# Feed-forward input of a two-layer model: tokens stationary, 512 weight columns moving, products in five units, values turned by VectorE and transfers

## The chip, the core and the metric

The kernel runs on one core of a Trainium2 chip. A core has TensorE (PE in the profile), VectorE (DVE), ScalarE (ACT), GpSimd (POOL) and SyncE (SP), which work beside one another, each through its own queue in order. The metric is the device time of one execution in microseconds. Before the change the median of three runs is 1403.25 us (1403.13 to 1403.97).

## The reference

512 tokens of width 1024 pass an attention layer, a feed-forward layer, an mLSTM layer, a second feed-forward layer and a last norm. All is float32. The change touches the first half of the feed-forward layers:

```
def rms_norm(x, g):
    y = xf * lax.rsqrt(jnp.mean(xf * xf, axis=-1, keepdims=True) + RMS_EPS)
    return y.astype(x.dtype) * g.astype(x.dtype)

def swiglu(xn, w_in, w_out):
    gu = xn @ w_in
    return (jax.nn.silu(gu[..., :D_FF]) * gu[..., D_FF:]) @ w_out

h = h + swiglu(rms_norm(h, ffn_norm[i]), ffn_w_in[i], ffn_w_out[i])
```

`w_in` has 1024 rows and 2 × 2816 columns (gates, then ups); `w_out` has 2816 rows and 1024 columns.

## The kernel before

Each float32 operand is split into a high part (written by ACT, `L207` for weights, `L225` for tokens) and a low part (DVE, `L208` and `L226`). A product is then three matmuls: high by high, high by low, low by high (`SPLITS`). A chunk of weights of 128x1024 numbers is loaded by SP, split, and held in one of three buffers for each of its raw, high and low forms (`W_BUFS`).

The residual `h` lies feature by feature: eight tiles `hx` (`hn` in layer 1) of 128 features by 512 tokens. `norm` (L1026) writes for each of the eight tiles the pair `n_h`, `n_l` (the tile times its gain, not yet divided by the root mean square) and its squares `n1sq`, which DVE adds into `n1ssum`. A step put off with `defer` multiplies `n1ssum` by ones on PE (`n1ss`, L1044), computes the inverse root, and a hook broadcasts it with two matmuls (`n1bc`, L328) into `rbc`, by which DVE later multiplies results.

`ffn_in` (L1057) computes gates and ups and their product `hid`, eleven tiles of two times 128 hidden values by 512 tokens. Weights are stationary and tokens move, so results stand hidden value by hidden value, as `ffn_out` wants them. Three column pairs (`PLAIN`) are plain products with 512 moving columns. The other eight column pairs are two-by-two blocks (gates and ups, upper and lower half of the features, two halves of the tokens), made with the seven products of Strassen's scheme in Winograd's form instead of eight (`PRODUCTS`): `A..` and `S..` are weight blocks and their sums (made by DVE, L1186), `B..` and `T..` token blocks and their sums, with 256 moving columns each.

`Halves` (L1297) does `ffn_out` in the same scheme, with three of the eleven tiles in plain products (`p0`, `p1`). Its weights are prepared two chunks ahead: `ffn_in` prepares with `AHEAD = 2`, and its last chunks already prepare the first of `ffn_out` (`unit.prepare`). `load` (L1311) brings a chunk with SP, or adds it to a buffer with an accumulating load of POOL (L1313).

A scheduler orders the instructions of each engine when the program is built, from the order of the code and its own estimate of times; the names of engines' rows below are as it left them. The following lines set the order of the chunks in `ffn_in`:

```
for n, (j, i) in enumerate(todo):
    prepare(n + AHEAD)
    if i == 0:
        steps_of = products(j, prepared[j][1])
    steps_of[i]()
```

The functions as they were:

Of the kernel before, what the change touches and what calls it, by code (L numbers as in the profile page):

```python
# [17 lines left out]
P = 128  # L18
# [52 lines left out]
def tile_hybrid_dilated_attn_mlstm(  # L71
# [954 lines left out]
    def norm(key, k0, name, gate=None):  # L1026
        pair = x_tiles(name)
        ssum = npl.tile([P, SEQ], F32, tag="ssum", name=name + "ssum")
        for k in range(KC):
            with tc.issue_after(gate) if gate is not None else nullcontext():  # L1030
                split_act(pair[0][k], pair[1][k], h[k], col(key, k0 + k))
                if k == 0:
                    nc.scalar.activation(ssum, h[k], AF.Square)
                else:
                    sq = npl.tile([P, SEQ], F32, tag="sq", name=name + "sq", bufs=2)
                    nc.scalar.activation(sq, h[k], AF.Square)
                    nc.vector.tensor_tensor(ssum, ssum, sq, op=ALU.add)
# [3 lines left out]
        def sums():  # L1041
# [5 lines left out]
            box["finish"]()  # L1047
        rbc, r, hook = inverse_rms(v, name, box)
        defer(1, sums)
# [3 lines left out]
    PRODUCTS = (("A11", "B11"), ("S1", "T1"), ("S2", "T2"), ("A12", "B21"), ("S3", "T3"), ("S4", "B22"), ("A22", "T4"))  # L1053
    PLAIN = 6
    AHEAD = 2

    def ffn_in(layer, fp, pair, rbc, hook, unit):  # L1057

# [4 lines left out]
        banks = itertools.cycle(("acc", "acc", "acc", "s", "s", "o", "o"))  # L1063

        def bank(name):
            tag = next(banks)
            return ps.tile([P, 512], F32, tag=tag, name=name, bufs=3 if tag == "acc" else 2)

        def place(i, name, dtype):
            p, tag = (xp, "x%d" % (i - 3)) if 3 <= i < 11 else (fp, "hid%d" % i)  # L1070
            return p.tile([P, 2, SEQ], dtype, tag=tag, name="f%d%s%d" % (layer, name, i))

        def hidden(i):
            return place(i, "hid", F32)

        def temp(tag, name, bufs=1):
            return fp.tile([P, SEQ], F32, tag=tag, name=name, bufs=bufs)

        def op_tile(i, name):
            return fp.tile([P, 4, HALF], F32R, tag="op%d" % i, name="f%d%s" % (layer, name))  # L1080


        ops, raw = {}, {}

        def split_tokens(key):
            i = [b for _, b in PRODUCTS].index(key)
            hi, lo = ops[key] = [op_tile(2 * i + part, key + "hl"[part]) for part in range(2)]
            nc.scalar.activation(hi, raw[key], AF.Copy)
            nc.vector.tensor_tensor(lo, raw[key], hi.bitcast(F32), op=ALU.subtract)

        def normalized():
            xs = [fp.tile([P, 4, SEQ], F32, tag="w8", name="f%dx%d" % (layer, i), bufs=2) for i in range(2)]
            for i in range(2):
                for t in range(2):
                    raw["B%d%d" % (i + 1, t + 1)] = xs[i][:, :, t * HALF:(t + 1) * HALF]
            for k in range(KC):
                nc.vector.scalar_tensor_tensor(xs[k // 4][:, k % 4], h[k], col("ffn", layer * KC + k), rbc,
                                               op0=ALU.mult, op1=ALU.mult)
                yield
            split_tokens("B11")  # L1100
            raw["T1"] = fp.tile([P, 4, HALF], F32, tag="t1", name="f%dt1" % layer)
            nc.vector.tensor_tensor(raw["T1"], raw["B12"], raw["B11"], op=ALU.subtract)
            yield

            raw["T3"] = raw["B12"]
            nc.vector.tensor_tensor(raw["T3"], raw["B22"], raw["B12"], op=ALU.subtract)
            split_tokens("T1")
            yield
            split_tokens("T3")
            yield  # L1110
            split_tokens("B22")
            yield
            raw["T2"] = raw["B22"]
            nc.vector.tensor_tensor(raw["T2"], raw["B22"], raw["T1"], op=ALU.subtract)
# [12 lines left out]

        def some(n):
            for _ in itertools.islice(steps, n):
                pass  # L1130


        chunks = [(j, ch, half) for j in range(0, PLAIN, 2) for ch in range(KC // 4) for half in range(2)]
        ready = []

        def split_next():
            if chunks:
                j, ch, half = chunks.pop(0)
                ready.append(split_chunk(weight_chunk(wi, ch, half * D_FF + j * P, 4, "f%dj%d_%d%d" % (layer, j, half, ch))))

        def plain(j):
# [4 lines left out]
            for ch in range(KC // 4):  # L1146
                for half in range(2):
# [804 lines left out]
```

## Time and profile before

| what | us |
|---|---|
| median of the runs | 1403.25 |
| profiled execution, its own time | 1403.12 |
| its span | 1401.3 |
| `ffn_in` of layer 0 on PE | from 489.10 to 717.09 |
| `ffn_in` of layer 1 on PE | from 1052.20 to 1280.63 |

The profile is one execution. A row of groups names line, engine, operation, `out<-in`, partitions by elements and the count, then busy time in us, mean of one in ns, and the idle time ahead of it with what ended it. A row of the chain has start, length and what. A row of the timeline has start, length, engine, line, and in brackets the idle time before it with its releaser. The span is the time from the first to the last instruction; the execution's own time has 1.8 us more around it. The granted clock of TensorE was 0.999.

### The profile page before, as it was taken

Reading aid. Unit: us, or ns where it says so; the run is one execution under the profiler, and the core shown is the slowest. Engines: PE = TensorE matmul, PEld = TensorE weight load, DVE = VectorE, ACT = ScalarE, POOL = GpSimd, SP = SyncE. Lnnn points to the kernel's source line nnn. Section 1 sums busy time; section 2 is a strip of 40 time slices with the busy share of each in tenths; the row PEclk is TensorE's granted clock in tenths of the full one; section 3 lists DMA queues with packets and bytes.
Section 4 is the critical chain, followed back from the end, with each engine's and each line's share of the span. In section 5 each row is a group of like instructions: output and inputs, shape, how many; then the busy total and the mean of one; then the engine's idle time right before and its main releaser. Section 6 shows DMA issues by size and latency. Waiting matters only on the chain.

```text
span 1401.3 us, 20914 instructions
## 1 busy us (share of the span) xinstructions
PE 1387.5 (99%) x8118; PEld 1226.5 (88%) x8118; DVE 1085.5 (77%) x1834; ACT 681.9 (49%) x1127; POOL 114.6 (8%) x161
## 2 busy tenths in 40 slices
PE   9999999999999999999999999999999999999997
PEld 7788888888888888999999988798888899999886
DVE  7976659687797687778798688987758778789865
ACT  7245553232325443444574554985534344457534
POOL 1014101000010100000012010100000000001322
PEclk9999999999999999999999999999999999999999
DMA  9538734427262423323586433221232432337762
GB/s 300 150 75 197 197 110 112 153 82 249 75 203 76 118 91 121 121 82 101 151 238 136 92 108 93 88 61 61 75 97 90 130 119 63 121 121 202 190 135 75
DMA packets 134379, 177.21 MB, mean 126 GB/s; under 512 B 7748, under 2 KB 98948, under 8 KB 134280
## 3 DMA queue, kind: packets, MB, share of 16 engines
q1 hardware_dynamic: 118320, 140.15, 32.0%
q0 software_dynamic: 13728, 33.86, 11.5%
q10 hardware_dynamic: 2232, 1.86, 0.5%
q8 instruction: 64, 1.05, 0.3%
q14 instruction: 35, 0.29, 0.1%
HBM read 162.19 MB, written 10.09 MB: 123 GB/s over the span
## 4 chain that ended last, share of the span: by engine, by line
PE 91%; DVE 6%; ACT 1%; issue 1%; DMA 0%; ACTq 0%; DVEq 0%
PE f1j_u L1215 5%; PE f0j_u L1215 5%; PE f1j L238 5%; PE f0j L238 5%; PE f0j_p L1215 3%; PE f1j_p L1215 3%; PE f0j_c L1215 3%; PE f1j_c L1215 3%; PE awo L238 3%; PE mwo L238 3%; PE mqk L238 3%; PE o_o L1476 2%; PE mo L238 2%; PE o_o L1880 2%; PE o_acc L1894 2%; PE o_s L1476 2%
## 5 line engine op out<-in xcount | busy, mean ns | idle before, releaser
L238 PE MATMUL f1j<-n_h,f1j_h 128*128 128x512 f32 x96 | 37.5, 390 | 0.0
L238 PE MATMUL f0j<-n_h,f0j_h 128*128 128x512 f32 x96 | 37.5, 390 | 0.0
L238 PE MATMUL f1j<-n_h,f1j_l 128*128 128x512 f32 x96 | 37.4, 389 | 0.0
L238 PE MATMUL f0j<-n_h,f0j_l 128*128 128x512 f32 x96 | 37.4, 389 | 0.0
L238 PE MATMUL f0j<-n_l,f0j_h 128*128 128x512 f32 x96 | 37.4, 389 | 0.0
L238 PE MATMUL f1j<-n_l,f1j_h 128*128 128x512 f32 x96 | 37.4, 389 | 0.0
L1313 POOL DMA_DIRECT2D o1own<-in_ffn_w_out_dram x8 | 9.8, 1238 | 286.9 <-DVE o1B L1360 258.5
L1313 POOL DMA_DIRECT2D o0own<-in_ffn_w_out_dram x8 | 10.2, 1309 | 265.7 <-PE f0j_u L1215 226.7
L523 DVE TENSOR_TENSOR rot<-rot,sinr 32x1024 f32<-32x1024 f32 x24 | 28.9, 1205 | 0.0
L238 PE MATMUL mo<-n_h,mo_k_h 128*128 128x512 f32 x64 | 25.4, 397 | 0.0
L238 PE MATMUL mo<-n_h,mo_k_l 128*128 128x512 f32 x64 | 25.2, 394 | 0.0
L238 PE MATMUL mo<-n_l,mo_k_h 128*128 128x512 f32 x64 | 25.2, 394 | 0.0
L238 PE MATMUL awo<-ao_h,awo_k_h 128*128 128x512 f32 x64 | 25.2, 396 | 0.0
L238 PE MATMUL mqk<-n_h,mqk_k_h 128*128 128x512 f32 x64 | 25.1, 392 | 0.0
L238 PE MATMUL mqk<-n_l,mqk_k_h 128*128 128x512 f32 x64 | 25.1, 392 | 0.0
L238 PE MATMUL awo<-ao_l,awo_k_h 128*128 128x512 f32 x64 | 25.0, 390 | 0.0
L238 PE MATMUL mqk<-n_h,mqk_k_l 128*128 128x512 f32 x64 | 25.0, 390 | 0.0
L238 PE MATMUL awo<-ao_h,awo_k_l 128*128 128x512 f32 x64 | 24.9, 392 | 0.0
L238 PE MATMUL mwo<-yo_h,mwo_k_h 128*128 128x512 f32 x64 | 24.9, 389 | 0.0
L238 PE MATMUL mwo<-yo_l,mwo_k_h 128*128 128x512 f32 x64 | 24.9, 389 | 0.0
L238 PE MATMUL mwo<-yo_h,mwo_k_l 128*128 128x512 f32 x64 | 24.9, 389 | 0.0
L1476 PE MATMUL o_o<-o0T,o0s_h 128*128 128x256 f32 x128 | 23.4, 285 | 0.0
(2319 smaller groups left out, 5413.8 us busy)
## 6 DMA issues: line engine op xcount, KB each, us to landing
f0j_w<-in_ffn_w_in_dram SPq DMA_DIRECT2D x28, 512.0 KB, 4.3
f1j_w<-in_ffn_w_in_dram SPq DMA_DIRECT2D x28, 512.0 KB, 4.0
o0a_w<-in_ffn_w_out_dram SPq DMA_DIRECT2D x12, 512.0 KB, 4.0
o1a_w<-in_ffn_w_out_dram SPq DMA_DIRECT2D x12, 512.0 KB, 8.6
awo_k_w<-in_attn_w_out_dram SPq DMA_DIRECT2D x8, 512.0 KB, 4.0
o0own<-in_ffn_w_out_dram POOLq DMA_DIRECT2D x8, 512.0 KB, 9.1
mv_k_w<-in_mlstm_w_in_dram SPq DMA_DIRECT2D x8, 512.0 KB, 4.2
mqk_k_w<-in_mlstm_w_in_dram SPq DMA_DIRECT2D x8, 512.0 KB, 3.6
```

Of the source, the lines that this page charges most:

```text
L238: nc.tensor.matmul(acc, whl[a][:, k, m * P:(m + 1) * P], pairs[b][kk], start=(kk == 0 and (a, b) == SPLITS[0]), stop=(kk == nk - 1 and (a, ...
L523: nc.vector.tensor_tensor(sh, sh, sinr.unsqueeze(1).to_broadcast([R, 2, SEQ]), op=ALU.mult)
L1215: nc.tensor.matmul(acc[name][:, m * HALF:(m + 1) * HALF], whl[a][:, k, m * P:(m + 1) * P], ops[okey][b][:, k], start=(fresh and m == 0 and ...
L1313: nc.gpsimd.dma_start(view, self.source(col, ch), accum_op=ALU.add)
L1476: nc.tensor.matmul(dst[m // 2][:, (m % 2) * HALF:(m % 2 + 1) * HALF], whl[a][:, k, m * P:(m + 1) * P], unit.form(okey, b, 2 * c + k), star ...
L1880: nc.tensor.matmul(dst[t], unit.form(okey, a, 2 * c + k)[:, t * P:(t + 1) * P], whl[b][:, k], start=(first and k == 0 and (a, b) == SPLITS ...
L1894: nc.tensor.matmul(rest[n][tb], unit.plain[c][a][k][:, tb * P:(tb + 1) * P], whl[b][:, k], start=(c == 0 and (n == 1 or tb >= 2) and k == ...
```

## The change

`norm` gets `rows=True` for the feed-forward layers. The tokens of a tile are then reordered as they are written: token 4x + o goes to column 128 o + x, so that each of four blocks of 128 columns holds every fourth token. The step between neighbouring numbers on one side of these instructions is 16 bytes. The inverse root stays a value per token (`r`, and `nr` with a minus), and `hook` and `rbc` are gone.

In `ffn_in` tokens are now stationary and weights move with 512 columns. First come four chunks `rest` for the last 256 gate and 256 up columns, in plain products over four token blocks. Then come five units of 512 gate and 512 up columns, each with seven products in two chunks of twelve matmuls. `a..` and `s..` are the weight blocks and sums: `begin` loads a11 and a21 and adds a22 to the latter with POOL's accumulating load; the others are made by DVE (L1120, L1123) and a further accumulating load (L1121). `token_forms` makes the token sums from scaled copies of `h`, `f0x` (L1144).

Results stand token by token. They are multiplied by `r` or `nr`, a value for each partition, and the product of gate and up must be turned for `ffn_out`: `turn` has DVE transpose blocks of 32x32 (L1181), written with a step of 16 bytes, and `spread` brings the blocks to their partitions, four by copies of POOL (L1188) and twelve by transfers of SP (L1190). The last unit is spread in two halves, 24 transfers. In `Halves`, tile 10 becomes the first plain one (`PLAIN_AT`), and some buffers move.

The diff, cut:

```diff
-    def norm(key, k0, name, gate=None):
+    by_rows = lambda t: t.rearrange("p (o x) -> p x o", o=TB)
+    by_time = lambda t: t.rearrange("p (x o) -> p x o", o=TB)
+    def norm(key, k0, name, gate=None, rows=False):
...
-                split_act(pair[0][k], pair[1][k], h[k], col(key, k0 + k))
+                split_act(to(pair[0][k]), to(pair[1][k]), of(h[k]), col(key, k0 + k))
...
-                    nc.scalar.activation(sq, h[k], AF.Square)
+                    nc.scalar.activation(to(sq), of(h[k]), AF.Square)
...
+        todo = [("rest", None, c) for c in range(KC // 2)] + [
+            (u, key, c) for u in range(UNITS) for key, _ in PRODUCTS for c in range(2)]
...
+            for c in range(2):
+                nc.sync.dma_start(quarter(raw["first", c]), weights(u, "a11", c))
+            for c in range(2):
+                nc.sync.dma_start(quarter(raw["own", c]), weights(u, "a21", c))
+                nc.gpsimd.dma_start(quarter(raw["own", c]), weights(u, "a22", c), accum_op=ALU.add)
...
+            if key == "s1":
+                nc.vector.tensor_tensor(own, own, first, op=ALU.add)
+                nc.gpsimd.dma_start(quarter(first), weights(u, "a21", c), accum_op=ALU.add)
+            elif key == "s2":
+                nc.vector.tensor_tensor(own, own, raw["a12", c], op=ALU.add)
...
+        def turn(to, o, src, n):
+            nc.vector.transpose(to.rearrange("p g n j o -> p o n g j")[:, o], src.rearrange("p (n x) -> p n x", n=n))
+        def spread(dest, src, first=0):
+            for a, g in itertools.product(range(TB), repeat=2):
...
+                if a == g:
+                    nc.gpsimd.tensor_copy(to, of)
+                else:
+                    nc.sync.dma_start(to, of)
...
+            else:
+                g = kept["g", t]
+                nc.vector.scalar_tensor_tensor(g, banks["u"][t], nr[:, t:t + 1], g, op0=ALU.mult, op1=ALU.mult)
+                turn(kept["to"], t, g, 4)
...
+                for t in range(2):
+                    for k in range(2):
+                        for a, b in SPLITS:
+                            nc.tensor.matmul(banks[name][t], tokens(dict(PRODUCTS)[key], a, 2 * c + k, t), whl[b][:, k],
...
-            if i % 2:
-                advance()
...
+            advance()
+            if n > 0:
+                next(forms, None)
...
+    PLAIN_AT = (10, 8, 9)
...
-                self.load(raw, place[0], place[1] + c)
+                self.load(raw, place[0], PLAIN_AT[c] if key[0] == "p" else place[1] + c)
```

Three places where the order of instructions moves. The first is ACT at the start of layer 0's feed-forward, from the first square on (`awo` are weights of the projection before, `hx` the residual's tiles). Before:

```order
L1033 ACTIVATE n1ssum<-hx_2836 128x512
L1036 ACTIVATE n1sq<-hx_2837 128x512
L207 ACTIVATE awo_k_h<-awo_k_w 128x1024
L1036 ACTIVATE n1sq<-hx_2838 128x512
L1036 ACTIVATE n1sq<-hx_2839 128x512
L207 ACTIVATE f0j_00_h<-f0j_00_w 128x1024
L1036 ACTIVATE n1sq<-hx_2840 128x512
L1036 ACTIVATE n1sq<-hx_2841 128x512
L225 ACTIVATE n_h_3903<-hx_2836,cols 128x512
L225 ACTIVATE n_h_3903<-hx_2837,cols 128x512
```

The same place after the change:

```order
L1037 ACTIVATE n1ssum<-hx_2836 128x128x4
L1040 ACTIVATE n1sq<-hx_2837 128x128x4
L1144 ACTIVATE f0x_4056<-hx_2836,cols 128x128x4
L1144 ACTIVATE f0x_4056<-hx_2837,cols 128x128x4
L207 ACTIVATE awo_k_h<-awo_k_w 128x1024
L1040 ACTIVATE n1sq<-hx_2838 128x128x4
L1040 ACTIVATE n1sq<-hx_2839 128x128x4
L1144 ACTIVATE f0x_4056<-hx_2838,cols 128x128x4
L207 ACTIVATE f0restNone_h<-f0restNone_w 128x1024
L1144 ACTIVATE f0x_4056<-hx_2839,cols 128x128x4
L1144 ACTIVATE f0x_4057<-hx_2840,cols 128x128x4
L1040 ACTIVATE n1sq<-hx_2840 128x128x4
```

Six scaled copies now stand among the squares. To the last square, from the `awo_k_h` just ahead of these rows on, the queue has 28 instructions: eight squares, six copies, eight `n_h` and six splits of 128x1024; before it had 21. On PE the matmuls of `n1ss` stand after 24 matmuls of the feed-forward layer in both programs.

The second is DVE where unit 1 of layer 0 ends and unit 2 begins (`f0u1` is unit 1, `f02a` are a11 and a12 of unit 2). Before, at the end of a column pair:

```order
L208 TENSOR_TENSOR f0j10A_l<-f0j_w_4842,f0j10A_h 128x1024
L1221 TENSOR_TENSOR f0j8g_4880<-f0j_p_4726,f0j8u_4781 128x512
L208 TENSOR_TENSOR f0j10S_l<-f0j10S,f0j10S_h 128x1024
L1254 TENSOR_TENSOR f0hid_4879<-f0j8v_4751,f0j8g_4880 128x2x256
L1186 TENSOR_TENSOR f0j10S<-f0j10S,f0j_w_4842 128x1024
L1258 TENSOR_TENSOR f0hid_4879<-f0j_u,f0j8g_4811 128x2x256
L208 TENSOR_TENSOR f0j10S_l<-f0j10S,f0j10S_h 128x1024
```

After:

```order
L1181 STREAM_TRANSPOSE f0u1turn<-f0u1up_4601 128x4x4x32
L1181 STREAM_TRANSPOSE f0u1turn<-f0u1up_4603 128x4x4x32
L208 TENSOR_TENSOR f02a_l<-f0u2w_4721,f02a_h 128x1024
L1235 SCALAR_TENSOR_TENSOR f0u1g_4561<-f0u_u,n1nr,f0u1g_4561 128x512
L1235 SCALAR_TENSOR_TENSOR f0u1g_4563<-f0u_u,n1nr,f0u1g_4563 128x512
L1181 STREAM_TRANSPOSE f0u1turn<-f0u1g_4561 128x4x4x32
L1181 STREAM_TRANSPOSE f0u1turn<-f0u1g_4563 128x4x4x32
L208 TENSOR_TENSOR f02a_l<-f02a_w,f02a_h 128x1024 x2
```

The two products (L1235) and two turns that end a unit now stand ahead of the low parts of the next unit's a12 (last row). POOL's four copies L1188 and SP's twelve transfers L1190 wait for the last of these turns.

The third is SP where `ffn_in` of layer 0 ends and `ffn_out` begins (`o0p_w` are the weight chunks of the first plain product p0, `o0own` and `o0first` other weights of `ffn_out`). Before:

```order
L1315 DMA o0first_6569<-in_ffn_w_out_dram 128x2x512 x2
L1315 DMA o0a_w<-in_ffn_w_out_dram 128x2x512 x3
L1315 DMA o0p_w<-in_ffn_w_out_dram 128x2x512
L1315 DMA o0own_6282<-in_ffn_w_out_dram 128x2x512
L1315 DMA o0own_6323<-in_ffn_w_out_dram 128x2x512
L1315 DMA o0p_w<-in_ffn_w_out_dram 128x2x512 x2
```

After:

```order
L1312 DMA o0first_5997<-in_ffn_w_out_dram 128x2x512
L1312 DMA o0p_w<-in_ffn_w_out_dram 128x2x512
L1190 DMA f0hid_5666<-f0u4turn 32x2x128 x12
L1190 DMA f0hid_5683<-f0u4turn 32x2x128 x12
L1312 DMA o0p_w<-in_ffn_w_out_dram 128x2x512 x2
L1312 DMA o0own_5786<-in_ffn_w_out_dram 128x2x512 x2
```

The 24 transfers of the last unit stand between the first and the second chunk of p0. In layer 1 the rows are the same (`o1p_w`, `f1u4turn`).

More of the change, by code (lines that the diff above doesn't have):

```diff
@@ L1047, in sums, with finish @@
             box["finish"]()
+        defer(1, sums)
+        if rows:
+            r, nr = (npl.tile([P, TB], F32, tag="rtok", name=name + n, bufs=2) for n in ("r", "nr"))
+            def finish():
+                nc.vector.tensor_scalar(v, v, 1.0 / D, EPS, op0=ALU.mult, op1=ALU.add)
+                rsqrt_newton(npl, v, TB, name + "r", r)
+                nc.vector.tensor_scalar(nr, r, -1.0, None, op0=ALU.mult)
+            box["finish"] = finish
+            return pair, r, nr
         rbc, r, hook = inverse_rms(v, name, box)
-        defer(1, sums)
@@ L1050, in norm, with ffn_in @@
         return pair, rbc, r, hook
-    PRODUCTS = (("A11", "B11"), ("S1", "T1"), ("S2", "T2"), ("A12", "B21"), ("S3", "T3"), ("S4", "B22"), ("A22", "T4"))
-    PLAIN = 6
+    PRODUCTS = (("a11", "B11"), ("a12", "B21"), ("s1", "T1"), ("s2", "T2"), ("s3", "T3"), ("s4", "B22"), ("a22", "T4"))
+    UNITS = D_FF // 512
     AHEAD = 2
-    def ffn_in(layer, fp, pair, rbc, hook, unit):
+    def ffn_in(layer, fp, pair, r, nr, unit):
         wi = ffn_w_in[layer]
[L1063 to L1102, printed above, removed]
@@ new lines, in prepare @@
+        def prepare(n):
+            if n >= len(todo):
+                unit.prepare(n - len(todo))
+                return
+            u, key, c = todo[n]
+            name = "%s%s%s%d" % (nm, u, key, c)
+            if u == "rest":
+                src = wp.tile([P, 1024], F32, tag="wraw", name=name + "_w", bufs=W_BUFS)
+                for half in range(2):
+                    c0 = half * D_FF + UNITS * 512
+                    nc.sync.dma_start(src.rearrange("p (k g n) -> p k g n", k=2, g=2)[:, :, half],
+                                      wi[2 * c * P:2 * (c + 1) * P, c0:c0 + 256].rearrange("(k p) n -> p k n", p=P))
+                made[n] = split_chunk((src, 1024, quarter, name))
+                return
+            if (key, c) == ("a11", 0):
+                begin(u)
+            first, own = raw["first", c], raw["own", c]
+            if key in ("a12", "a22"):
+                src = raw[key, c] = wp.tile([P, 1024], F32, tag="wraw", name=name + "_w", bufs=W_BUFS)
+                nc.sync.dma_start(quarter(src), weights(u, key, c))
+            else:
+                src = first if key in ("a11", "s3") else own
+            made[n] = split_chunk((src, 1024, quarter, name))
+            if key == "s1":
[3 more added lines that the diff above has]
+                nc.vector.tensor_tensor(own, own, raw["a12", c], op=ALU.add)
@@ L1261, in ffn_in @@
[L1261 to L1275 removed]
+            nc.vector.tensor_tensor(half1(x2), half2(x2), half1(x2), op=ALU.subtract)
@@ new lines, in ffn_in, with rest_out @@
+        hid = unit.hid = [None] * (FC // 2)
+        def rest_out(accs):
+            hid[-1] = fp.tile([P, 2, SEQ], F32, tag="hid10", name=nm + "hid10")
+            to = turned(2, "rest")
+            for o in range(TB):
+                g = wide(("g2", "up")[o // 2], "gr%d" % o, 256)
+                nc.scalar.activation(g, accs[o][:, :256], AF.Silu, scale=r[:, o:o + 1])
+                nc.vector.scalar_tensor_tensor(g, accs[o][:, 256:], r[:, o:o + 1], g, op0=ALU.mult, op1=ALU.mult)
+                turn(to, o, g, 2)
+            spread(hid[-1], to)
@@ L1469, in tile_hybrid_dilated_attn_mlstm @@
                        25: (("T4", 3),)}, {"p1": 3}, ("a22",), ("s2",))
-        ffn_in(0, fp, pair, rbc, hook, unit)
+        ffn_in(0, fp, pair, r, nr, unit)
         whole = {}
```

306 lines of the change are left out of this document (139 added, 167 removed).

## The prediction

> **What bounds the kernel now.** I read the page first, then the chain that ended last, then the two feed-forward inputs by windows. The page says that TensorE never rests and that its clock is whole:
>
> ```profile
> span 1401.3 us, 20914 instructions
> PE 1387.5 (99%) x8118; PEld 1226.5 (88%) x8118; DVE 1085.5 (77%) x1834; ACT 681.9 (49%) x1127; POOL 114.6 (8%) x161
> PEclk9999999999999999999999999999999999999999
> ```
>
> The windows below cut each layer's `ffn_in` into its plain pairs and its seven-product pairs, layer 0 and then layer 1. The columns are length, busy time of PE, weight load, DVE, ACT and POOL, clock, DMA share, GB/s:
>
> ```profile
> 489.10:555.82 66.72, 66.72 (x300) 55.33 (x300) 53.56 (x80) 26.36 (x31) 0.00 (x0) 1.00 0.36 111
> 555.82:717.09 161.27, 161.27 (x1347) 161.27 (x1346) 129.83 (x131) 85.23 (x109) 2.44 (x2) 1.00 0.40 116
> 1052.20:1118.92 66.72, 66.72 (x301) 55.33 (x300) 53.55 (x80) 26.35 (x31) 0.00 (x0) 1.00 0.36 111
> 1118.92:1280.63 161.71, 161.71 (x1350) 161.71 (x1349) 130.49 (x131) 85.51 (x110) 1.20 (x1) 1.00 0.36 110
> ```
>
> PE is busy in every microsecond of all four. So the stage costs what its matmuls cost, 227.99 us in layer 0 and 228.43 in layer 1, and anything that makes PE wait there is added in full. The chain gives the pace of each kind (start, length, what):
>
> ```profile
> 489.10 5.44 PE f0j L238 x24
> 494.54 0.79 PE n1ss L1044 x8
> 495.32 8.34 PE f0j L238 x36
> 503.66 0.47 PE n1bc L328 x2
> 558.70 2.88 PE f0j_p L1215 x24
> 847.17 10.90 PE mv L296 x48
> ```
>
> A matmul of 512 columns takes 5.44/24 = 226.7 ns and one of 256 columns 2.88/24 = 120 ns. The mv row has tokens stationary and weights moving, as the change has, and 512 columns: 10.90/48 = 227.1 ns. Turning the operands round is therefore free.
>
> **The matmuls.** Before, a layer has 288 of 512 columns and 1344 of 256: 65.3 + 161.3 us, and with the two small rows (0.79 and 0.47) that is the two windows. After, it has 96 for the rest and 5 × 7 × 24 = 840 for the units, all of 512 columns: 936 × 226.7 = 212.2 us. The four sums of n1ss stay (0.79), the broadcast n1bc goes. So 213.0 instead of 227.99 and 228.43: **−15.0 and −15.4, together −30.4 us**. What is late next is everything that feeds PE, at three places.
>
> **The head: squares behind more and slower work.** PE's order has n1ss after 24 matmuls, before and after, so PE waits there until the eighth square is summed. ACT's queue in layer 0, and what its instructions cost:
>
> ```profile
> 472.55 1.06 ACT L207 ACTIVATE awo_k_h<-awo_k_w 128x1024 fp32r<-128x1024 f32 x1 [2.04 <-PE awo L238]
> 491.19 0.62 ACT L1036 ACTIVATE n1sq<-hx 128x512 f32<-128x512 f32 x1
> L225 ACT ACTIVATE n_h<-hx,cols 128x512 fp32r<-128x512 f32 x8 | 5.3, 712 | 0.3 <-PE awo L238 0.3
> L1510 ACT ACTIVATE hn<-hx x4: 1129/1142/1147, 801.4 to 807.2; 128x512 f32<-128x512 f32 x4
> L1500 DVE TENSOR_TENSOR hn<-o_acc,hx x3: 1060/1064/1066, 819.6 to 827.0; 128x512 f32<-128x512 f32 x3
> L1037 DVE TENSOR_TENSOR n1ssum<-n1ssum,n1sq 128x512 f32<-128x512 f32 x7 | 4.8, 687 | 0.3
> ```
>
> Today the last square ends at 491.81, long before PE asks at 494.54. The change rewrites every square and every n_h with a step of 16 bytes, and puts six scaled copies f0x and a split of T1 ahead of the last square. L1510 and L1500 write with that step too: 1142 ns against the 620 of n1sq, and 1064 against the 687 of L1037. From 472.55 to the last square stand 22 stepped instructions and six splits of 128x1024. Eight n_h are busy for 5.3 us and not for 8 × 0.712, so instructions of a row overlap by some 0.08; at 1.06 and 0.97 us each the queue is 23.3 + 5.8 = 29.1 us and ends at 501.7 without a single wait; with waits on PE and DVE as in the timeline I take 503. The last sum (0.69) and n1ss (0.79) follow: PE goes on at about 504.5 instead of 495.32. **+9 us**, bounds 0 (stepped writes cost nothing extra) and 12 (with a wait of 2.04, as that of the first row, more).
>
> Layer 1 has its residual spread over 43 us, so most squares are early. From the first n_h:
>
> ```profile
> 1045.44 1.34 ACT L225 ACTIVATE n_h<-hn,cols 128x512 fp32r<-128x512 f32 x2 [2.66 <-PE mwo L238]
> 1056.03 0.69 DVE L1037 TENSOR_TENSOR n3ssum<-n3ssum,n3sq 128x512 f32<-128x512 f32 x1
> 1058.43 8.34 PE f1j L238 x36
> ```
>
> Behind 1045.44 stand eight n_h, two squares, one f1x and two splits: 11 × 1.06 + 1.9 = 13.6, so 1059.0; the sum and n3ss bring PE to 1060.6 if ACT is alone, and some 1.5 later with DVE's eight n_l at 1.06 between them. Against 1058.43: **+3 us**, bounds 0 and 6.
>
> **Inside the units.** A unit takes PE 168 × 0.2267 = 38.1 us. Its feeding, by these rows:
>
> ```profile
> L208 DVE TENSOR_TENSOR f0j_l<-f0j_w,f0j_h 128x1024 fp32r<-128x1024 f32 x5 | 6.1, 1222 | 1.1 <-ACT f0j_h L207 1.0
> L226 DVE SCALAR_TENSOR_TENSOR n_l<-hx,cols,n_h 128x512 fp32r<-128x512 f32 x8 | 5.8, 747 | 0.2 <-ACT n_h L225 0.2
> L870 DVE STREAM_TRANSPOSE a0pB<-a0p x2: 2162/2168/2173, 231.4 to 235.9; 128x1920 f32<-128x1920 f32 x2
> L876 POOL COPY a3pT<-a3pB x8: 575/580/588, 454.3 to 458.7; 32x480 f32<-32x480 f32 x8
> 1280.63:1311.10 30.47, 30.47 (x150) 25.40 (x149) 25.08 (x36) 16.92 (x26) 4.82 (x6) 1.00 0.96 273
> ```
>
> DVE: 14 splits and 4 sums at 1.22, 8 products at 0.75, 4 turns. L870 gives 1.13 ns an element, 0.58 us for 512, when it writes in one run; the new turns write with a step of 16 bytes, which no transpose of the trace does. Bounds 0.58 and, with L1510's 522 ns on top, 1.10; I take 1.0, since L1510 and L1500 have the step and L870 has not. Sum 22.0 + 6.0 + 4.0 = 32 of 38.1 us, so DVE keeps pace. DMA: 12 loads of 512 KB and 0.8 MB of turned values a unit, 7.1 MB in 38.1 us, 186 GB/s, below the 273 that the last row shows. The sums of weights that accumulating loads now make have these rows:
>
> ```profile
> L1313 POOL DMA_DIRECT2D o0own<-in_ffn_w_out_dram x8 | 10.2, 1309 | 265.7 <-PE f0j_u L1215 226.7
> o0own<-in_ffn_w_out_dram POOLq DMA_DIRECT2D x8, 512.0 KB, 9.1
> ```
>
> The tightest is that for s3: s1's split comes two chunks ahead of its matmuls, some 6 us after the unit's start, DVE's sum 1.2 later, 1.31 to issue, 9.1 to land: 17.6, and s3's split is due at 8 chunks of 2.72 less 2.3, at 19.5. All of these loads lie beside PE's work with some 2 us in hand and are charged nothing; where that is gone, each of ten units pays the lateness whole.
>
> The tight point is the **join of two units**. At a unit's end E, DVE does two products and two turns, then the low part of the next a12's first chunk; PE wants it after a11, 24 × 0.2267 = 5.44 us later. The first product can start before E, so: E + 0.2 + 0.75 + 2.0 + 1.22 = E + 4.2, with semaphores up to 5.5. **+1 us** for all eight joins, bounds 0 and 20 (below).
>
> **The tail: loads behind the turned values.** After the last unit SP issues 24 transfers that wait for the last turn (E + 0.2 + 0.75 + 2.0 = E + 2.95), and only then the second and third weight chunks of p0. Rows:
>
> ```profile
> L878 SPq DMA_DIRECT2D a3pT<-a3pB x12: 507/592/824, 454.2 to 461.7; - x12
> o0p_w<-in_ffn_w_out_dram SPq DMA_DIRECT2D x6, 512.0 KB, 4.5
> 717.09 11.52 PE o_acc L1476 x96
> 734.08 1.36 PE o_acc L1490 x6
> 1280.63 2.75 PE o_acc L1880 x12
> 1294.70 1.39 PE o_acc L1894 x6
> ```
>
> E is 717.09 today, and the second chunk of p0 begins at 734.08, E + 17.0. 24 × 0.592 = 14.2 puts the load at E + 17.2, its landing (4.5) at 21.7, and a split of high (1.06) and low (1.22) part at E + 24.0: **+7 us**. Bounds: 0.507 each and a turn of 0.58 give 3.6; at the 0.66 that 8.01 us for twelve would make, 8.7. In layer 1 PE has the transposed residual in between: E is 1280.63, p0 begins at 1294.70 and its second chunk 5.44 later, E + 19.5, so 2.5 less: **+4.5**, bounds 1 and 6.5.
>
> **Sum**, against the profiled execution's own 1403.12 us (its span 1401.3; the median of the runs shown is 1403.25, nothing between them): −30.4 + 9 + 3 + 1 + 7 + 4.5 = −5.9, so **1397 us**. With head and tail 8 us better or worse together it is 1389 to 1405; 0.2%, 2.8 us, is what a measurement here can tell from no change.
>
> **Rivals.**
>
> (a) *The fillers cost little.* Stepped writes cost ACT and DVE nothing, the last square is as early as now, SP issues at 507 ns. For: ACT is idle 51% of the span. Against: L1510 and L1500 both show the step's price. Head 1, joins 0, tail 3.6 + 1: −24.8, **1378**.
>
> (b) *Slower: the joins are late.* Place: eight joins, where four POOL copies of 32 x 512 (0.58 each by L876, whose rows have 480) become due in the moment in which DVE must make the low part of a12. The trace has one such meeting:
>
> ```profile
> 1324.39 2.26 DVE L208 TENSOR_TENSOR o1s_l<-o1own,o1s_h 128x1024 fp32r<-128x1024 f32 x1
> 1324.15 1.42 POOL L1853 TENSOR_TENSOR ht<-ht,gbc 128x512 f32<-128x512 f32 x1 [1.62 <-ACT fsq L1852]
> ```
>
> A split that otherwise takes 1.22 us took 2.26 beside a POOL instruction. If all four copies go first, the low part comes at E + 4.2 + 2.3 = 6.5, with one more microsecond of its own 7.5: 1.1 to 2.1 beyond the 5.44; with the later semaphores of the term above 1.4 to 2.5. It decides from 5.44 on; eight times that is 11 to 20 us, so 1407 to 1416, **1411**. Against: a copy starts from a semaphore, the split stands on the same engine as the turn and can be first.
>
> The rule that would make this: the Trainium skill, SBUF — State Buffer, section SBUF: two separate sides, says that VectorE with two SBUF inputs and a GpSimd instruction reading SBUF share a port pair of which the first holds the whole. The two rows at 1324 agree; whether four short copies in a row keep VectorE out, no run here shows.
>
> (c) *The matmuls don't do what the count says.* The slowest piece of the kind that has weights moving is
>
> ```profile
> 831.06 5.55 PE mv L296 x24
> ```
>
> which is 231 ns and not 227. If all new matmuls ran so: 1872 × 4.3 ns = 8 us, **1405**. Against: 24 of f0j and 48 of mv in a row run at 227.
>
> **How the numbers follow.** The forecast, stalls at head and tail that eat four fifths of the gain, 0.50 (0.42 faster, 0.08 the same). (a) 0.18, all faster. (b) 0.24 (0.21 slower, 0.03 the same). (c) 0.08 (0.05 the same, 0.03 slower). Faster 0.60, same 0.16, slower 0.24. The range 1378 to 1415 leaves out the lower half of (a) and the upper third of (b), with the tails of the others about 0.2.
>
> **What would show it.** Matmuls: groups of 840 and 96 at 226.7 ns a layer. Head: PE idle before n1ss, released by the sum of squares on DVE, about 9 and 3 us; ACT's stepped instructions at 1.1 us. Joins: PE idle before the a12 matmuls of each next unit, and the DVE split beside POOL's copies. Tail: SP's 24 issues without a break, the second p0 load behind them, PE idle before its matmuls, 7 and 4.5 us. Wrong it would be if PE ran through the head (then a), if a load or an accumulating load of POOL arrives late inside a unit (nothing is charged for it), or if the joins wait more than 1.1 us each.

## The result, and the profile after

The change makes the kernel slower: median 1428.11 us of four runs (1426.92 to 1428.43) against 1403.19 (1403.09 to 1403.97), a ratio of 1.0175 with a 95% interval of 1.0162 to 1.0187. The profiled execution took 1428.43 us, 25.3 more than that of before. The forecast was 1397.0 with a range of 1378 to 1415.

The page of after:

```profile
span 1426.6 us, 18608 instructions
PE 1375.5 (96%) x6722; PEld 1152.7 (81%) x6722; DVE 1098.4 (77%) x1816; ACT 731.5 (51%) x1165; POOL 230.3 (16%) x257
PEclk9999999999999989999999999999999999999999
```

PE has 1396 instructions fewer, but it is now idle for 51 us of its span (14 before), and the row of the granted clock, all nines before, has an 8 where layer 0's rest stands (slice 15). The windows of after, cut on PE's timeline into layer 0's sums (until `n1ss`, `n1ss` itself, the other 72 matmuls of the rest), its units, and the start of `ffn_out` up to the second chunk of p0 and then up to p0's end; columns as in the prediction:

```profile
490.14:503.12 12.98, 6.16 (x25) 4.16 (x24) 12.37 (x15) 11.87 (x14) 0.00 (x0) 0.82 0.14 40
503.12:504.85 1.73, 1.73 (x8) 1.73 (x9) 1.73 (x2) 1.73 (x3) 0.00 (x0) 0.50 0.03 9
504.85:523.04 18.19, 18.19 (x73) 14.89 (x74) 14.74 (x30) 8.04 (x10) 0.00 (x0) 0.90 0.19 58
523.04:720.16 197.12, 192.41 (x842) 156.81 (x840) 163.08 (x165) 109.12 (x133) 48.92 (x39) 1.00 0.68 175
720.16:748.86 28.70, 17.95 (x122) 15.87 (x120) 22.25 (x32) 11.30 (x17) 6.84 (x9) 0.92 0.65 172
748.86:762.45 13.59, 13.59 (x48) 10.98 (x49) 6.77 (x7) 3.20 (x4) 2.41 (x2) 0.80 1.06 304
```

The same six pieces of layer 1:

```profile
1069.39:1079.04 9.65, 5.60 (x25) 4.35 (x24) 8.19 (x10) 9.54 (x10) 0.00 (x0) 0.98 0.17 51
1079.04:1080.74 1.70, 1.70 (x8) 1.70 (x9) 0.99 (x1) 0.68 (x1) 0.00 (x0) 0.50 0.74 274
1080.74:1099.39 18.65, 18.65 (x73) 15.23 (x74) 13.22 (x28) 7.11 (x9) 0.00 (x0) 0.87 0.10 29
1099.39:1295.57 196.18, 192.56 (x842) 156.74 (x841) 163.11 (x165) 109.66 (x134) 48.97 (x39) 1.00 0.68 176
1295.57:1323.19 27.62, 20.33 (x106) 16.67 (x104) 22.30 (x32) 14.63 (x25) 13.83 (x12) 0.96 0.70 190
1323.19:1336.36 13.17, 13.17 (x49) 10.68 (x49) 6.49 (x6) 3.18 (x3) 4.13 (x3) 0.83 1.06 303
```

Set against the matmul counts of the prediction at 226.7 ns and against the same tail before (717.09 to 744.96 and 1280.63 to 1311.02), this gives the losses:

| place | loss, layer 0 | layer 1 | of both: waits and what they delay | of both: half clock | forecast |
|---|---|---|---|---|---|
| sums and rest (22.55 by count; layer 0 also starts 1.0 late) | 11.4 | 7.45 | 12.8 | 6.05 | 12 |
| five units (190.4) | 6.7 | 5.8 | 12.5 | 0 | 1 |
| start of `ffn_out` (27.87, 30.39) | 14.4 | 10.4 | 19.8 | 5.0 | 11.5 |

The half clock is worked out from pieces without a wait: `n1ss` 1.73 and 1.70 instead of 0.79, 72 matmuls in 18.19 and 18.65 instead of 16.32, and the last two chunks of p0 in 13.59 and 13.17 instead of 10.88. The column before it is the loss without the half clock. PE stands idle for 10.9, 8.3 and 18.0 us of it; the rest is the late start and matmuls that begin later than their pace around a wait, while the one before them still counts as busy. All losses are 56.1 us; with the matmuls' -30.4 that makes +25.7, of 25.3 measured.

PE's waits of after, by what it waited for (us in total, times, longest):

```profile
PE o_acc L1483 <- ACT o0p_h L207: 9.9, 2, 9.5
PE n1ss L1048 <- DVE n1ssum L1041: 6.8, 1, 6.8
PE o_acc L1888 <- ACT o1p_h L207: 6.5, 1, 6.5
PE n3ss L1048 <- DVE n3ssum L1041: 4.0, 1, 4.0
PE f0u_u L1273 <- ACT f0u1g L1205: 1.8, 1, 1.8
PE f1u_u L1273 <- ACT f1u2g L1205: 1.7, 1, 1.7
PE f0u_u L1273 <- ACT f0u4g L1205: 1.2, 1, 1.2
PE f0u_u L1273 <- ACT f0u3g L1205: 1.2, 1, 1.2
PE f1u_u L1273 <- ACT f1u4g L1205: 1.1, 1, 1.1
PE f0u_p L1273 <- DVE f04s_l L208: 0.6, 1, 0.6
```

The four long waits are the two heads and the two tails. The short ones stand inside the units, nearly all at one place: ACT's copies of s2's result (`L1205`), which free the bank that s3's matmuls need. The last row, a wait for a split of s1, is in the fifth unit; layer 1's fifth unit has one of 0.6 as well. By the starts of the matmuls s3 loses 9.5 us in all, the fifth units' s1 and s2 2.4, and the eight joins, where the list has no wait, 0.5.

### The profile page after: what moved, and what is told of

It is laid out like the page before. It is cut to its first block, busy times and chain, and to the rows that moved or that the text cites. A ratio compares the mean times of both kernels' runs of the same rounds, so it can differ in the third digit from the quotient of the medians.

```text
span 1426.6 us, 18608 instructions
## 1 busy us (share of the span) xinstructions
PE 1375.5 (96%) x6722; PEld 1152.7 (81%) x6722; DVE 1098.4 (77%) x1816; ACT 731.5 (51%) x1165; POOL 230.3 (16%) x257
## 3 DMA queue, kind: packets, MB, share of 16 engines
q10 hardware_dynamic: 2232, 1.86, 0.5%
## 5 line engine op out<-in xcount | busy, mean ns | idle before, releaser
L1469 PE MATMUL o_acc<-o0B,o0a_h 128*128 128x256 f32 x128 | 23.3, 284 | 0.0
L208 DVE TENSOR_TENSOR o1a_l<-o1a_w,o1a_h 128x1024 fp32r<-128x1024 f32 x12 | 15.3, 1271 | 10.3 <-ACT o1a_h L207 10.3
L208 DVE TENSOR_TENSOR o0a_l<-o0a_w,o0a_h 128x1024 fp32r<-128x1024 f32 x12 | 14.8, 1237 | 10.0 <-ACT o0a_h L207 10.0
L1694 POOL CAST ql<-ql 64x512 fp32r<-64x512 f32 x8 | 7.1, 890 | 94.4 <-DVE ql L1693 94.3
L207 ACT ACTIVATE o0a_h<-o0a_w 128x1024 fp32r<-128x1024 f32 x12 | 12.7, 1055 | 18.9 <-PE o_s L1483 6.7
L207 ACT ACTIVATE o1a_h<-o1a_w 128x1024 fp32r<-128x1024 f32 x12 | 12.7, 1057 | 18.8 <-PE o_acc L1888 6.2
L207 ACT ACTIVATE o0s_h<-o0own 128x1024 fp32r<-128x1024 f32 x12 | 12.7, 1058 | 18.2 <-PE o_s L1469 6.3
L1874 PE MATMUL o_acc<-o1a_h,o1B 128*128 128x512 f32 x64 | 20.8, 394 | 0.0
```

Of the source, the lines that this page charges most:

```text
L207: nc.scalar.activation(hi[:, :n], raw[:, :n], AF.Copy)
L208: nc.vector.tensor_tensor(lo[:, :n], raw[:, :n], hi[:, :n].bitcast(F32), op=ALU.subtract)
L1469: nc.tensor.matmul(dst[m // 2][:, (m % 2) * HALF:(m % 2 + 1) * HALF], whl[a][:, k, m * P:(m + 1) * P], unit.form(okey, b, 2 * c + k), star ...
L1694: nc.gpsimd.tensor_copy(ql[oth], ql[own].bitcast(F32))
L1874: nc.tensor.matmul(dst[t], unit.form(okey, a, 2 * c + k)[:, t * P:(t + 1) * P], whl[b][:, k], start=(first and k == 0 and (a, b) == SPLITS ...
```

## The experiments

Each run shares its runs of before (medians 1403.4 to 1403.8); "after" is 1428.1.

**Does the idle time itself slow the clock?** PE's wait before the sums is filled with matmuls whose result nobody reads.

```diff
+            if rows:
+                dum = ps.tile([P, 512], F32, tag="t", name=name + "dum", bufs=1)
+                for _ in range(28 if name == "n1" else 16):
+                    nc.tensor.matmul(dum, pair[0][0][:, :P], pair[0][0], start=True, stop=True)
```

> Ahead of the sum-of-squares matmuls (n1ss, n3ss) TensorE gets 28 and 16 products of 512 columns whose result is used nowhere; they fill the idle time there (6.8 and 4.0 us), nothing else changes. Theory A (an idle TensorE is granted half the clock, and keeps it for some microseconds after it works again): the idle time stays as it is, but the 72 matmuls of the rest behind it take 16.3 us and not 18.2 and 18.7, and n1ss 0.8 and not 1.7: about 6 us less than the changed kernel's 1428.1, so 1422, and the clock is 1.00 there. Rival B (the slow matmuls behind the gaps wait for operands): no gain, 1428.

Measured 1422.17 (ratio 1.0132, 1.0117 to 1.0147), 5.9 us less than after, as much as the half clock of both heads by the table, 6.05. Windows of this kernel in layer 0:

```profile
501.00:505.00 4.00, 3.39 (x19) 2.69 (x18) 3.97 (x5) 3.94 (x5) 0.00 (x0) 1.00 0.00 0
505.00:509.00 4.00, 4.00 (x19) 3.29 (x18) 4.00 (x5) 1.29 (x2) 0.00 (x0) 1.00 0.51 148
```

PE does more work, none of it useful, and the clock stays at 1.00 where after had 0.50; the sums come no earlier. Theory A holds. So the wait costs twice: once as a wait, once in the matmuls behind it.

**Do three chunks of the rest hide the squares?**

```diff
-        defer(1, sums)
+        defer(3 if rows else 1, sums)
```

> The sum-of-squares matmuls stand behind three chunks of the rest and not behind one. Theory A: the wait for the squares goes, and the half clock with it: 6.8 + 2.8 us in layer 0 and 4.0 + 3.2 in layer 1, about 17 less, 1411. Rival B (the clock is none of it): 11 less, 1417. Rival C (the inverse root is then late for the rest's results, and the wait moves there): less than 8 less.

Measured 1417.19 (1.0102, 1.0082 to 1.0123), 10.9 us less. The number is rival B's, but not for its reason. In layer 1 the whole loss of the head is gone: 72 matmuls of the rest in 16.32 us, sums 0.80. In layer 0 the head takes 27.80 us instead of 32.90, still 5.25 more than by count, since another wait appears, on the low part of the rest's next chunk:

```profile
PE f0rest L1257 <- DVE f0restNone_l L208: 2.4, 1, 2.4
```

DVE starts that split at 502.55, though ACT had its high part ready at 499.56: ahead of it on DVE stand three stepped `n_l` (from 498.43, 3.64 us) and a sum of squares. The 72 matmuls ahead of the sums take 21.41 us and not 16.32, a half clock of 3.4 us behind the wait (504.04 to 507.45) among it. So theory A holds in layer 1, and in layer 0 a new wait takes half of the gain.

**Do the scaled copies belong behind the squares?** They are made to follow on ACT.

```diff
+              with tc.issue_after(last_on(mybir.EngineType.Activation)):
                 for k in ks:
                     nc.scalar.activation(by_rows((x1, x2)[k // 4][:, k % 4]), by_time(h[k]), AF.Copy,
...
```

> The scaled copies f0x may not stand ahead of ACT's work that the program wrote before them: they go behind n_h and the squares, which keep their stepped writes. Theory A (six copies and the split of T1 ahead of the last square hold it up): 7.4 us less ahead of it in layer 0, so the wait of 6.8 and the half clock behind it (2.8) go, and a microsecond ahead of the rest; in layer 1 one or two copies less, the wait of 4.0 falls to about 2: 1428.1 less 12, 1416. Rival B (the stepped writes of squares and n_h alone make the last square late): 3 less at most.

Measured 1435.03 (1.0227, 1.0206 to 1.0247), 6.9 us more than after, where both theories had less. PE's waits in this kernel:

```profile
PE n1ss L1048 <- DVE n1ssum L1041: 3.4, 1, 3.4
PE f0u_u L1274 <- ACT f0u0g L1206: 2.0, 1, 2.0
```

In layer 1 the same two are 3.1 and 1.9. The wait for the sums is shorter by 3.4 and 0.9 us, but not early enough to keep the clock, and the first unit of each layer, which took its 38.08 without a wait, now has one of 2.0 at s3 and one of 1.4 before its second product, both for ACT. The second four copies now start at 519.26, behind the results of the rest in ACT's queue, and the unit's copies and splits come behind them; yet ACT stood idle for 4.2 and 4.4 us ahead of them. It is the order in the queue that decides who is late.

**What do the stepped writes cost?** Tokens and squares are written in one run, and the matmuls read every fourth token.

```diff
-        of, to = (by_time, by_rows) if rows else (lambda t: t, lambda t: t)
+        of, to = lambda t: t, lambda t: t
...
-                            nc.tensor.matmul(accs[o], pair[a][2 * c + k][:, o * P:(o + 1) * P], whl[b][:, k],
+                            nc.tensor.matmul(accs[o], by_time(pair[a][2 * c + k])[:, :, o], whl[b][:, k],
```

> n_h, n_l and the squares are written in one run again, in the order of time, and TensorE reads every fourth token as its stationary operand; the copies f0x stay as they are, ahead of the last square. Theory A (stepped writes cost 0.5 us each, 16 of them ahead of the last square, 7.4 us): the wait in layer 0 and its half clock go as in the other run, and most of layer 1's: 1428.1 less 12 to 15, 1413 to 1416. Rival B (a stationary operand read with a step of 16 bytes loads more slowly than a matmul takes): the rest and the four products on n_h take longer than 226.7 ns a matmul, and the kernel is slower than 1428.

Measured 1420.51 (1.0126, 1.0111 to 1.0141), 7.6 us less, between theory A and rival B, which both hold in part. The wait of 6.8 us before `n1ss` falls to 0.5: the step was what made the squares late. But a matmul whose stationary tokens are read with the step takes 235 ns (48 in 11.28 us), 8 more than 226.7, and a layer has 96 + 5 × 72 = 456 of them: 3.8 us. And in layer 1 the clock falls all the same:

```profile
1067.00:1070.00 3.00, 3.00 (x14) 3.00 (x14) 1.95 (x4) 1.77 (x2) 0.00 (x0) 1.00 0.41 143
1070.00:1073.00 3.00, 3.00 (x9) 2.43 (x9) 3.00 (x7) 1.06 (x1) 0.00 (x0) 0.52 0.21 38
```

PE counts as busy throughout. The sums before it are eight matmuls of one column, which here take 1.86 us: the page calls that busy, but the array streams next to nothing. In layer 0, where the sums took as long, the clock did not fall; the last section has what tells the two apart.

**Are the units slowed by POOL's copies?** Whole units are spread by 16 transfers of SP.

```diff
-                if a == g:
+                if a == g and dest.shape[1] == 2:
                     nc.gpsimd.tensor_copy(to, of)
```

> In the units that are spread whole, the four copies of POOL become four more transfers on SP (16 a unit and not 12); the rest and the last unit keep theirs. Theory A (POOL's copies hold up POOL's accumulating loads and VectorE beside them, so the weights of s3 come late, ACT waits for them and TensorE for ACT): the waits at s3 go, 7 to 9 us less than 1428.1, about 1420. Rival B (the accumulating loads are late by their own issue and landing): 2 less at most.

Measured 1422.57 (1.0136, 1.0119 to 1.0152), 5.5 us less, nearer to theory A. The waits of s3 for `L1205` fall from 7.3 us over all units (the rows of after and one of 0.3) to 3.7, and only the fifth units have them; the units are 6.8 us shorter. Two rows of groups of after, with the copies and the splits of unit 1 of layer 0:

```profile
L1188 POOL COPY f0hid<-f0u1turn 32x512 f32<-32x512 f32 x4 | 6.0, 1491 | 8.6 <-DVE f0u1turn L1181 8.4
L208 DVE TENSOR_TENSOR f01s_l<-f0u1w,f01s_h 128x1024 fp32r<-128x1024 f32 x8 | 10.4, 1297 | 6.6 <-ACT f01s_h L207 6.4
```

and the second of them without the copies:

```profile
L208 DVE TENSOR_TENSOR f01s_l<-f0u1w,f01s_h 128x1024 fp32r<-128x1024 f32 x8 | 9.8, 1224 | 6.0 <-ACT f01s_h L207 6.0
```

A copy takes 1.49 us where 0.58 was taken, and DVE's splits beside them 1.30 on average instead of 1.22. The single copies of after show why. With DVE at rest (from 729.88) one of half the size takes 0.39 us. At the joins DVE's split starts first, and each copy ends 0.47 or 0.48 us behind the end of DVE's instruction beside it (567.12 after 566.65, 568.67 after 568.20); DVE's next one then starts beside that end and is up to 0.4 us longer. So it is the copies that wait for DVE, and what they delay in turn is POOL's own accumulating loads, which stand behind them in its queue.

**Is the rest of the units' loss an order on ACT?** ACT's timeline in unit 1 of layer 0 of after:

```profile
577.69 0.69 ACT L1205 ACTIVATE f0u1up<-f0u_p,n1nr 128x512 f32<-128x512 f32 x1 [0.67 <-PE f0u_p L1273]
578.28 1.05 ACT L207 ACTIVATE f01s_h<-f0u1w 128x1024 fp32r<-128x1024 f32 x1
583.17 1.06 ACT L207 ACTIVATE f01s_h<-f0u1w 128x1024 fp32r<-128x1024 f32 x1 [3.84 <-PE f0u_u L1273]
584.13 1.25 ACT L1205 ACTIVATE f0u1g<-f0u_u,n1r 128x512 f32<-128x512 f32 x2
```

POOL's timeline ahead of it, with the copies of unit 0 and the two accumulating loads for s3 of unit 1:

```profile
565.67 6.11 POOL L1188 COPY f0hid<-f0u0turn 32x512 f32<-32x512 f32 x4 [7.11 <-DVE f0u0turn L1181]
571.84 1.18 POOL L1121 DMA_DIRECT2D f0u1w<-in_ffn_w_in_dram  x1
575.63 1.21 POOL L1121 DMA_DIRECT2D f0u1w<-in_ffn_w_in_dram  x1 [2.61 <-issue]
```

The issues of after between 560 and 600 us have a row for these two, the last number being the time from issue to landing:

```profile
f0u1w<-in_ffn_w_in_dram POOLq DMA_DIRECT2D x2, 512.0 KB, 6.8
```

The split at 583.17 is s3's second chunk. Its wait is put down to PE, whose matmul had long been done; what it waited for is the second accumulating load, issued at 575.63, which lands 6.8 later by the median, at 582.4. For s3's own second chunk, half of s3's 5.44 us later than the first, that need not be late. But s2's copies stand behind it on ACT, and s3's first chunk needs their bank: PE waits 1.8 us. The edit lets the copies go first:

```diff
-            prepare(n + AHEAD)
+            late = (key, c) == ("s2", 1)
+            if not late:
+                prepare(n + AHEAD)
...
+            if late:
+                with tc.issue_after(last_on(mybir.EngineType.Activation)):
+                    prepare(n + AHEAD)
```

> Only the order on ScalarE inside a unit is changed: the split of s3's second chunk is prepared behind the two copies of s2, so that ScalarE's row is s3's first split, s2's two copies, s3's second split. Theory (the units lose their time because s2's copies stand behind a split that waits for the accumulating load of s3's second chunk): the waits of s3's matmuls for L1205, 7.3 us over the ten units before, fall to below 2 us in all, and the time to about 1422. Rival A (s3's first load is as late as its second, so the first split holds the copies just the same): the waits stay within 1 us of 7.3, the time stays at 1427 to 1429. Rival B (the wait is only handed on, from the copies to s3's second chunk): the waits for L1205 go and waits of the same length for that split (f04s_l, f14s_l and the like) come, the time stays above 1426.

Measured 1424.20 (1.0142, 1.0125 to 1.0159), 3.9 us less. The waits for `L1205` are gone but for the fifth units':

```profile
PE f1u_u L1275 <- ACT f1u4g L1205: 1.3, 1, 1.3
PE f0u_u L1275 <- ACT f0u4g L1205: 1.3, 1, 1.3
```

7.3 us have become 2.6, without touching POOL, SP or the loads. The units are 5.1 us shorter (194.05 and 194.11 against 197.12 and 196.18), of which layer 1's tail gives back 1.8; the time is 2 above the theory's 1422. Rivals A and B are out. The fifth units keep their waits because the edit does not reach them: ACT's row there, in layer 0, still has the split (698.69) ahead of the copies (699.66 and 700.75). The split is held behind the last instruction that ACT was given before it, and in the fifth units that is one of `ffn_out`'s, not a copy.

**Is it SP's queue that makes p0 late?** SP in the tails of after, layer 0 and layer 1:

```profile
725.60 17.83 SPq L1190 DMA_DIRECT2D f0hid<-f0u4turn  x24
743.53 1.05 SPq L1312 DMA_DIRECT2D o0p_w<-in_ffn_w_out_dram  x2
...
1300.92 16.83 SPq L1190 DMA_DIRECT2D f1hid<-f1u4turn  x24
1317.84 1.05 SPq L1312 DMA_DIRECT2D o1p_w<-in_ffn_w_out_dram  x2
```

As forecast, 24 transfers without a break and p0's loads behind them. They begin 5.4 us after the last unit (720.16), for this on DVE:

```profile
719.17 2.05 DVE L1181 STREAM_TRANSPOSE f0u4turn<-f0u4up 128x512 f32<-128x512 f32 x2
721.04 1.23 DVE L208 TENSOR_TENSOR o0a_l<-o0a_w,o0a_h 128x1024 fp32r<-128x1024 f32 x1
722.18 1.39 DVE L1235 SCALAR_TENSOR_TENSOR f0u4g<-f0u_u,n1nr,f0u4g 128x512 f32<-128x512 f32 x2
723.49 2.08 DVE L1181 STREAM_TRANSPOSE f0u4turn<-f0u4g 128x512 f32<-128x512 f32 x2
```

The two last products wait behind the turns of the ups and a split for `ffn_out`. In one kernel these two loads go through ACT's queue; in another the second half's 12 transfers go behind them (a step of `ffn_out` that needs the second half moves a chunk later).

```diff
...
+                self.load(raw, place[0], PLAIN_AT[c] if key[0] == "p" else place[1] + c,
+                          queue=nc.scalar if key == "p0" and c > 0 else nc.sync)
```

> The second and third weight chunk of the first plain product of ffn_out are issued from ACT's queue and so no longer stand behind the 24 transfers on SP. Theory (the load behind the transfers sets the tail): TensorE's waits of 9.6 and 6.8 us fall to about 2 and 0, and the half clock behind them goes (2.7 and 2.3): 19 less than 1428.1, so 1409. Rival (the turned values of the last unit, 24 transfers in 17 us, are themselves what is late): 3 less at most.

```diff
-                        spread(hid[i], kept["to"], 2 * (i - 2 * u))
+                    spread(hid[2 * u], kept["to"], 0)
+                    unit.late_spread = lambda to=kept["to"]: spread(hid[2 * u + 1], to, 2)
...
+                    self.late_spread()
+                    self.load_own(2)
```

> The second half of the last unit's transfers (12 of 24) is issued behind the loads of p0's second and third weight chunks and not ahead of them. Theory (the load behind the transfers sets the tail, and SP's issue is the queue): the load is issued some 8 us earlier; TensorE's waits fall from 9.6 to about 2 in layer 0 and from 6.8 to 0 in layer 1, with the half clock (2.7 and 2.3): 19 less than 1428.1, 1409. Rival (the turned values themselves are late): the wait moves to the third chunk's tokens, and less than 8 is gained.

The first took 1419.07 (1.0129, 1.0097 to 1.0162), with runs from 1414.11 to 1427.86, 9 us less and not 19: the rival is out, and the theory's time is missed by 10. Layer 0's long wait goes, layer 1 gets a new one:

```profile
PE o_acc L1889 <- ACT ht L1820: 4.8, 1, 4.8
```

ACT's timeline shows what stands ahead of `ht`:

```profile
1291.28 5.34 ACTq L1312 DMA_DIRECT2D o1p_w<-in_ffn_w_out_dram  x2
```

ACT's queue is held for 5.34 us by two issues, and what stands behind them waits. The second took 1414.71 (1.0083, 1.0066 to 1.0100), 13.4 us less than after; its waits for p0 fall from 9.9 to 2.7 us in layer 0 and leave the list in layer 1. The rival is out here too; the theory's 1409 is missed by 6. Of what this saves, about 3.5 us is clock: of the 5.0 of the table a half clock of 3.4 us (741.48 to 744.89), behind the wait that is left, still costs 1.5.

**Together.** The first kernel has the later sums, the scaled copies behind the squares, SP's transfers and the late half. The second and the third add ACT's order from the units' experiment and give six of the first half's 12 transfers to ACT's queue; the third leaves the scaled copies as in the change.

> Four edits together: copies f0x behind the squares, sum-of-squares matmuls behind three chunks of the rest, POOL's copies as transfers in the whole units, the second half of the last unit's transfers behind p0's loads. Theory (the stalls at head, units and tail, with the half clock behind them, are all that the change loses, and add up): 1428.1 less 18 (head), 5 (units) and 19 (tail), 1386, some 17 faster than before. Rival (a stall that is mended comes back at the next place that waits): between 1395 and 1410.

> Five edits together: the sums for the normalisation behind three chunks of the rest, all eight scaled copies behind the squares on ScalarE, s3's second split behind s2's copies, whole units' rows moved by SP's transfers alone, and the first half's 12 transfers of the last unit divided between SP's and ScalarE's queues with the second half's 12 behind p0's loads. Theory (the stalls are separate and each edit removes its own): against the version without the third edit and the division (1402.5), the units give up some 5 us and the tails some 5 more, 1390 to 1396. Rival (the transfers that ScalarE issues hold its splits of p0 as they held the others): the tails gain nothing or lose up to 4, 1397 to 1406.

> The same five edits but for the one on the scaled copies, which stay where the change put them. Theory A (behind the squares they make the first unit late by as much as they save the squares, which three chunks of the rest hide anyway): 2 to 6 us less than with that edit. Theory B (layer 0 needs the squares early even behind three chunks, where 4.7 of the head's loss was left to win): 2 to 5 us more than with it.

They took 1402.45 (0.9991, 0.9982 to 1.0000), 1404.14 (1.0008, 0.9999 to 1.0018) and 1400.12 (0.9980, 0.9968 to 0.9991). The theories' 1386 for the first and 1390 to 1396 for the second missed; both times lie where the rivals had them. Moving the scaled copies costs 4.0 us, the difference of the last two (theory A): with them behind the squares the heads take 22.71 us in both layers, hardly more than the count, but the first units then wait. The transfers on ACT bring a new wait in layer 1:

```profile
PE hT L304 <- ACT ht L1827: 4.2, 1, 4.2
```

The last kernel keeps only the three edits that put no work on another queue: later sums, ACT's order in the units, the late half on SP.

> Three edits together, each of which was measured alone: the sums behind three chunks of the rest (-10.9 us), s3's second split behind s2's copies (-3.9), the second half's 12 transfers of the last unit behind p0's loads (-13.4). VectorE, GpSimd and SP share the rows of whole units as in the change, and ScalarE issues no transfer. Theory A (the three places are separate and the gains add): 1428.1 - 28.2 = 1399.9, between 1397 and 1402, just ahead of before. Theory B (what a stall hid comes out behind it, as with the scaled copies): 1403 to 1410. The version with SP's transfers in the units and ScalarE's in the tail gave 1400.1; theory C (those two edits were worth something of their own) makes this one 1402 or more, theory D (they cost as much as they gave, by the waits in the fifth units and for ht that came with them) leaves it at 1397 to 1401.

It took 1397.50 (1397.08 to 1400.51; ratio 0.9965, 0.9952 to 0.9979), its clock 0.997. The three gains add (28.2 forecast, 30.6 measured; theories A and D), and this version is 0.35% faster than before. The two longest of the waits that it still has in the places changed:

```profile
PE f0rest L1260 <- DVE f0restNone_l L208: 2.4, 1, 2.4
PE o_acc L1491 <- ACT o0p_h L207: 2.2, 2, 2.1
```

## Why the prediction was wrong

Three steps of the prediction failed: the clock behind a wait, put at nothing; the inside of the units, charged nothing; and the tail, sized too small.

- **Matmuls, -30.4: right.** Wherever nothing waits, 24 new matmuls take 5.44 us, 226.7 ns each. Rival (c), 231 ns, is out.
- **Head, +12: right.** Without the clock the heads lose 12.8, with ACT's stepped instructions as the cause; with plain writes the wait falls from 6.8 to 0.5.
- **The clock after a wait: the step that was missing.** The sum took a wait as its own length. The matmuls behind each of the four long ones ran at half clock for a while: 11.0 us. The page's row of the clock, all nines before, showed nothing of it, since before PE never waited there; the dummy matmuls showed it, and the version with them is 5.9 us faster, against the heads' 6.05.
- **Inside the units, "charged nothing": wrong, 12.5 us.** The prediction followed each accumulating load to the matmul that uses it and found 2 us in hand. It did not ask what stands behind the waiting split on ACT. There stand s2's copies, needed one chunk sooner. Changing only that order removes 4.7 of the 7.3 us of these waits. A second cause is the copies' price, 1.49 us and not 0.58, which puts the accumulating load later: without them 3.6 of the 7.3 are gone. An accumulating load that arrives late inside a unit is what the prediction had named as a sign of being wrong.
- **Joins, +1: right in size.** PE's list has no wait there, and the 48 matmuls that follow a join take 10.93 to 10.96 us instead of 10.88, 0.5 in all. So rival (b) had the sign, but not the mechanism, and its 1411 is 17 short: POOL's copies hurt through POOL's queue, not by keeping DVE from a12's low part. The rule of the Trainium skill named there (SBUF — State Buffer, section SBUF: two separate sides) the copies bear out, with the parts exchanged: at a join it is DVE that comes first, and each copy ends 0.47 or 0.48 us behind DVE's instruction.
- **Tail, +11.5: right mechanism, too small; 19.8 in waits.** The transfers start at E + 5.4 (725.60 - 720.16) and not E + 2.95, because both products and not one come behind the unit's end, with a turn and a split of `ffn_out` ahead of them on DVE, and they take 17.83 and 16.83 us, 0.74 and 0.70 each, above the upper bound of 0.66. Both together are 6.1 and 5.0 us more; the rest of the working was 1.4 too high in each layer. The lower bound of layer 0's term, given as 3.6, comes to 4.1 by its own figures; that decides nothing.

Of the 31 us between 1397.0 and 1428.1, the missing clock is 11.0, the units with their joins 11.5 and the tail 8.3.

Not settled: why an accumulating load for s3 takes anything from 5.6 to 8.3 us from its issue to its landing, and how much of the units' loss would be left if the new order held in the fifth units too.

## What to carry to other kernels

Where an instruction will wait, list what stands behind it on its engine and when each of these is due: the first to be late is often not the one whose data are late. A wait on PE of more than about 2 us has to be charged with the half clock behind it, so cutting a stall to well below that is worth more than its length. And a fix is tried alone first: those that moved work to another busy queue (ACT's issues, the copies behind the squares) moved the wait with it, while the three that only changed an order added up.

## What the hardware showed

The clock of PE fell to half after short waits. Windows of the version with transfers on ACT, around a wait of 2.1 us for s2's copies in layer 0's fifth unit:

```profile
694.00:697.00 3.00, 0.94 (x4) 0.71 (x4) 1.42 (x2) 2.51 (x4) 0.00 (x0) 0.95 0.81 272
697.00:700.00 3.00, 3.00 (x8) 2.32 (x8) 3.00 (x5) 1.69 (x3) 0.00 (x0) 0.50 0.00 0
```

The clock falls at 696.70, half a microsecond behind the end of the wait, and eight matmuls fit into 3 us where 13 do at full clock.

The traces hold when the granted clock changes. But for one that the end of the program cuts off, it is half only in stretches of 3.41, 6.83 or 10.24 us (in after 498.35 to 508.59, 744.11 to 754.35, 1078.61 to 1085.44 and 1320.96 to 1327.79), and the starts of any two of them in a run lie a multiple of 3.413 us apart. If all runs are cut into windows on that grid, from 480 to 1345 us, the clock fell only behind windows that held no more than about 6.0 matmuls of 512 columns (shorter ones, and those across a border, counted in part), and behind every one with less than 5.6; at full pace a window holds 15. So whether a wait of about 2 us costs clock depends on where it falls. In the version with dummy matmuls 1.9 us in unit 1 of layer 0 did (583.36 to 586.77) and 2.2 us in unit 3 did not; in the stages changed every wait of 2.4 us or more did. And the version with plain writes had 5.8 such matmuls in its window in layer 1, where the clock fell, and 6.3 in layer 0, where it did not.

The Trainium skill, TensorE: Matmul & The Clock Gate, section What's actually happening, has the halving, after at least one idle window of about 3.4 us. The halving and the length of the window agree; but the window need not be idle throughout, since 1.9 us of waiting in it were enough here.

A price beside it: stationary tokens read with a step of 16 bytes make a matmul of 512 columns 235 ns instead of 226.7.
